# The first two products of a four-layer trunk, begun chunk by chunk while x is being scaled

## The chip, the cores and the metric

One core of one Trainium2 chip runs the program. The metric is the device time of one execution in microseconds (us), as the median of several runs; less is better. TensorE (PE in the profile) multiplies matrices, its weight loads have rows of their own (PEld); VectorE is DVE, ScalarE is ACT, GpSimd is POOL. SyncE (SP) issues most transfers. Each engine takes its instructions in the order in which the program wrote them.

## What is computed

One step of a trunk of four layers over 128 context tokens and 512 latent tokens of width 1024. Each layer is a token mixer (attention, convolution, gated linear attention, attention again) and a gated FFN. Each of these has in front a norm and a modulation whose vectors come from a conditioning vector through a large matrix:

```python
for i in range(DEPTH):
    sh1, sc1, g1, sh2, sc2, g2 = adaln(cond, mod_w[i], mod_b[i])     # silu(cond) @ w + b, in six parts
    h = modulate(rms_norm(x, norm1_g[i]), sh1, sc1)                   # norm(x) * (1 + scale) + shift
    x = x + g1 * mixer(h)            # layer 0: attention, first step q, k, v = h @ w_qkv
    x = x + g2 * conv_ffn(modulate(rms_norm(x, norm2_g[i]), sh2, sc2))
```

## The kernel before

The tokens lie along the free dimension and the 1024 channels in 8 chunks of 128 partitions. A product is written as three: x and each weight are split into a rounded high part and a low rest (`xh`, `xl`, `wh`, `wl`), and for each chunk `proj` (line 207) issues six matmuls, two column halves of 320 and 322 by high times high, low times high, high times low. A product over 8 chunks is 48 matmuls into one of two PSUM tiles, `mm0` and `mm1`.

The norm's factor per token is applied after the product, so what stands in `xh` and `xl` is only x times `A`, a vector per channel (`1 + scale` times the norm's gain), and two more columns, 0 and 129, that hold the shift of the context and of the latent tokens. The product's columns 0 and 129 are then the shift's image, which is added as a bias after the norm's factor.

The program is one list of tasks (`build`, line 1648), each written out in turn for all engines. It begins thus: eight tasks `mod_unit` multiply the conditioning by the eight parts of the matrix that give the scale, four small matmul columns each in `b`; `mod_end` copies, transposes and sums the result, and forms `A`. Then `first_norm` scales all eight chunks of x (`fin`, line 257: ScalarE writes `xh`, DVE writes `xl`, ScalarE squares x and POOL or DVE adds the squares into `acc`). Then come eight `mod_unit` tasks for the shift, and `first_shift` writes the shift columns. Then `attention` (line 636) opens: for each of 8 pairs of heads the products q, k, v, one task each (`project`), with one more `mod_unit` of the coming vectors between them. Behind the first product stand the ones matmuls that sum the squares over the partitions, and the norm's factor (`norm_rstd`); each q and k is then normed over its head, for which TensorE sums the squares once more (`sb<-N,blk`).

Matrices come through a ring of four raw buffers `wr` in the order in which the tasks use them (`fill`, `advance`). x itself comes in four transfers, on the same queue, behind the eight of the scale. A weight is converted into a ring of four half buffers `wh` and `wl` (two halves make one weight): ScalarE casts, and DVE or, in attention, POOL subtracts. `advance` is called in the middle and at the end of each product and converts one more half ahead, if its buffer is not to be read any more by a matmul that is still to be written:

```python
wait = self.turn >= self.NWS and self.took[-self.NWS][0].left[self.took[-self.NWS][1]] > 0
if u >= get + need and (wait or limit == 0):
    return
```

Of the kernel before, what the change touches and what calls it, by code (L numbers as in the profile page):

```python
# [25 lines left out]
NCH = 8  # L26
# [99 lines left out]
class Trunk:  # L126
# [129 lines left out]

    def fin(self, j, A, rolled):

        nc = self.nc
        for src, dst, g in self.pieces(self.x[:, j], self.xh[:, j], rolled):  # L260
            nc.scalar.activation(out=dst, in_=src, func=AF.Copy, scale=A[:, j, g:g + 1])
        for (src, dst, g), (_, hi, _) in zip(self.pieces(self.x[:, j], self.xl[:, j], rolled),
                                             self.pieces(self.x[:, j], self.xh[:, j], rolled)):
            nc.vector.scalar_tensor_tensor(out=dst, in0=src, scalar=A[:, j, g:g + 1], in1=f32(hi), op0=ALU.mult,  # L264
                                           op1=ALU.subtract)
        self.square(j)

# [165 lines left out]

    def first_norm(self, perm):
        self.lane_a.drain()
        for j in range(NCH):
            self.fin(j, self.A[0], perm)

    def first_shift(self):
        self.lane_a.drain()  # L440
        self.shift_cols(self.mod[0][0][:])
        self.advance(0, 0, 2)

# [191 lines left out]

    def attention(self, layer, la):

# [254 lines left out]
        def project(w, p, which, first):  # L892
# [5 lines left out]
            if (which, p) == ("v", NCH - 1):  # L898
                self.lane_a.add(early())
            self.proj(pm, w, self.xmv, NCH, True)  # L900
            if first:
                self.norm_rstd(True, (S.SB, S.PB))
# [57 lines left out]
        for p in range(NCH):  # L960
            for w, which in enumerate("qkv"):
                main.append(Task(lambda w, p=p, which=which: project(w, p, which, p == 0 and which == "q"),
                                 [("w", self.i["w_qkv"][la, 3 * p + w])]))
        tasks = [self.open(f"att{layer}", build)]
        tasks += self.weave(main, self.mod_tasks(layer, [2, 3, 4]))
        tasks.append(Task(gap))
# [681 lines left out]
    def build(self, stack):  # L1648
# [4 lines left out]
        T += scale[:4] + [Task(self.load_x)] + scale[4:]  # L1653
        T.append(Task(lambda: self.first_norm(True)))
        T += self.mod_tasks(0, [0])
        T.append(Task(self.first_shift))
        na = 0
        for layer in range(self.depth):
            kind = layer % 3
            if kind == 0:  # L1660
                T += self.attention(layer, na)
                na += 1
# [138 lines left out]
```

## Time and profile before

| what | value |
|---|---|
| median of 3 runs | 3420.74 us (3420.28 to 3421.49) |
| the profiled execution | 3424.34 us, of which the span of its trace 3422.6 us |
| TensorE busy | 3325.3 us, 97% |
| VectorE, ScalarE, GpSimd busy | 58%, 49%, 19% |
| granted clock of TensorE, mean over the span | 0.989 of 2.4 GHz |

A share of the span is a mean over stages with different limits. The change touches the first 60 us of the program, so the rows below are nearly all of these. The granted clock is given in parts of 2.4 GHz: 0.50 is 1.2 GHz. In a timeline row the first number is the start, the second the busy time of the row's instructions, and the bracket at the end the idle time ahead of it with what ended it.

### The profile page before, as it was taken

The numbers are of one execution on the slowest core, as the hardware profiler recorded it, in microseconds if no ns is written. First come the engines' busy times: TensorE is split into PE (matmuls) and PEld (weight loads), VectorE is DVE, ScalarE is ACT, GpSimd is POOL, SyncE is SP. The second block draws the span as 40 slices with busy tenths as digits, with TensorE's granted clock in tenths as the row PEclk, the third lists the DMA queues.
The fourth block names the chain that finished last, engine by engine and source line by source line (L and its number), as shares of the span: only waits on it lengthen the run. The fifth ranks groups of instructions, "written<-read, shape, count | busy, mean of one in ns | idle before, by whom it ended". The sixth has DMA issues, their size and how long they took to land.

```text
span 3422.6 us, 58735 instructions
## 1 busy us (share of the span) xinstructions
PE 3325.3 (97%) x23852; PEld 3105.8 (91%) x23852; DVE 2002.1 (58%) x3395; ACT 1662.0 (49%) x3200; POOL 657.1 (19%) x597
## 2 busy tenths in 40 slices
PE   6999999999999899999999999999999999999999
PEld 4888899999977799999988899999998888999999
DVE  4555666465567666465566676646565555664654
ACT  5666555343413454343455555534357665543433
POOL 4443310000135210000233441000024443200000
PEclk8999999999999899999999999999999999999999
DMA  6333233332265333222332223333223333232222
GB/s 219 114 116 109 76 100 105 104 105 82 90 178 165 108 100 111 99 69 76 104 102 84 91 64 107 105 111 105 74 94 117 109 111 95 83 106 79 71 74 74
DMA packets 110928, 349.74 MB, mean 102 GB/s; under 512 B 14496, under 2 KB 19680, under 8 KB 110656
## 3 DMA queue, kind: packets, MB, share of 16 engines
q1 hardware_dynamic: 107856, 340.15, 31.0%
q0 software_dynamic: 2416, 5.13, 0.4%
q8 instruction: 188, 3.08, 0.4%
q10 hardware_dynamic: 384, 0.69, 0.1%
q14 instruction: 84, 0.69, 0.1%
HBM read 329.13 MB, written 5.77 MB: 98 GB/s over the span
## 4 chain that ended last, share of the span: by engine, by line
PE 59%; DVE 4%; ACT 4%; issue 1%; POOL 1%; DMA 0%; SPq 0%; DVEq 0%; ACTq 0%; POOLq 0%
PE mm L222 7%; PE mm L226 6%; PE mm L224 6%; PE mm L227 6%; PE mm L225 6%; PE mm L223 6%; PE ax L222 2%; PE ax L226 2%; PE ax L225 2%; PE ax L224 2%; PE ax L227 2%; PE ax L223 2%; PE b L342 1%; PE at L1451 1%; ACT Q L747 1%
## 5 line engine op out<-in xcount | busy, mean ns | idle before, releaser
L171 DVE TENSOR_TENSOR wl<-wr,wh 128x512 fp32r<-128x512 f32 (+1 forms) x555 | 387.9, 703 | 658.2 <-ACT wh L170 657.7
L170 ACT CAST wh<-wr 128x512 fp32r<-128x512 f32 (+2 forms) x802 | 472.7, 597 | 612.3 <-PE mm L225 335.9
L222 PE MATMUL mm<-xh,wh 128*128 128x320 f32 x1791 | 594.8, 332 | 5.7 <-ACT wh L170 3.1
L226 PE MATMUL mm<-xh,wl 128*128 128x320 f32 x1791 | 557.8, 311 | 2.8 <-POOL wl L171 2.8
L224 PE MATMUL mm<-xl,wh 128*128 128x320 f32 x1791 | 557.0, 311 | 3.6 <-DVE xl L264 2.4
L225 PE MATMUL mm<-xl,wh 128*128 128x322 f32 (+1 forms) x1791 | 558.5, 312 | 0.0
L223 PE MATMUL mm<-xh,wh 128*128 128x322 f32 (+1 forms) x1791 | 556.8, 311 | 0.0
L227 PE MATMUL mm<-xh,wl 128*128 128x322 f32 (+1 forms) x1791 | 556.7, 311 | 0.0
L171 POOL TENSOR_TENSOR wl<-wr,wh 128x512 fp32r<-128x512 f32 (+2 forms) x247 | 319.3, 1298 | 606.7 <-ACT wh L170 514.7
L222 PEld LDWEIGHTS mm<-xh,wh 128*128 128x128 f32 x1791 | 338.5, 189 | 68.1 <-issue 48.6
L223 PEld LDWEIGHTS mm<-xh,wh 128*128 128x128 f32 x1791 | 342.1, 191 | 5.9
L224 PEld LDWEIGHTS mm<-xl,wh 128*128 128x128 f32 x1791 | 338.5, 189 | 5.0 <-DVE xl L264 3.5
L226 PEld LDWEIGHTS mm<-xh,wl 128*128 128x128 f32 x1791 | 339.0, 189 | 3.4 <-POOL wl L171 3.4
L227 PEld LDWEIGHTS mm<-xh,wl 128*128 128x128 f32 x1791 | 341.6, 191 | 0.0
L225 PEld LDWEIGHTS mm<-xl,wh 128*128 128x128 f32 x1791 | 340.3, 190 | 0.0
L287 POOL TENSOR_TENSOR acc<-acc,T 128x640 f32<-128x640 f32 x40 | 64.9, 1622 | 1428.3 <-ACT T L285 1416.1
L491 ACT ACTIVATE U<-T,D 128x128 f32<-128x128 f32 x176 | 71.2, 405 | 503.2 <-DVE D L490 503.2
L797 ACT ACTIVATE T<-T,sm 128x512 f32<-128x512 f32 x128 | 92.7, 724 | 148.3 <-DVE sm L793 148.0
L500 ACT ACTIVATE y<-U,ffc 128x641 f32<-128x641 f32 x176 | 161.7, 919 | 0.0
L503 DVE SCALAR_TENSOR_TENSOR y<-U,ffc,y 128x641 f32<-128x641 f32 x176 | 156.4, 889 | 7.0
L502 DVE SCALAR_TENSOR_TENSOR y<-U,ffc,y 128x641 f32<-128x641 f32 x176 | 156.4, 889 | 3.6
L222 PE MATMUL ax<-xh,wh 128*128 128x320 f32 x480 | 150.4, 313 | 0.0
(377 smaller groups left out, 7465.7 us busy)
## 6 DMA issues: line engine op xcount, KB each, us to landing
wr<-in_mod_w SPq DMA_DIRECT2D x192, 512.0 KB, 4.3
wr<-in_w_up SPq DMA_DIRECT2D x176, 512.0 KB, 3.5
wr<-in_w_down SPq DMA_DIRECT2D x64, 448.0 KB, 3.4
wr<-in_w_qkv SPq DMA_DIRECT2D x48, 512.0 KB, 4.6
bias<-in_bias SPq DMA_DIRECT2D x64, 256.0 KB, 2.7
wr<-in_w_down SPq DMA_DIRECT2D x32, 512.0 KB, 3.7
cr<-cu SPq DMA_DIRECT2D x120, 84.0 KB, 3.0
wr<-in_w_ao SPq DMA_DIRECT2D x16, 512.0 KB, 3.9
```

Of the source, the lines that this page charges most:

```text
L170: self.nc.scalar.copy(out=h, in_=src[:, a:a + n])
L171: self.lo_eng[self.turn % len(self.lo_eng)].tensor_tensor(out=l, in0=src[:, a:a + n], in1=f32(h), op=ALU.subtract)
L222: mm(oa, wh, ha, start=st, stop=False)
L223: mm(ob, wh, hb, start=st, stop=False)
L224: mm(oa, wh, la, start=False, stop=False)
L225: mm(ob, wh, lb, start=False, stop=False)
L226: mm(oa, wl, ha, start=False, stop=en)
L227: mm(ob, wl, hb, start=False, stop=en)
L500: nc.scalar.activation(out=y[:], in_=u[:, 1:642], func=AF.Identity, scale=c[:, 2:3], bias=c[:, 4:5])
L502: stt(out=y[:], in0=u[:, 0:641], scalar=c[:, 1:2], in1=y[:], op0=ALU.mult, op1=ALU.add)
L503: stt(out=y[:], in0=u[:, 2:643], scalar=c[:, 3:4], in1=y[:], op0=ALU.mult, op1=ALU.add)
L797: nc.scalar.activation(out=st[:, a * w:a * w + w], in_=src[:, a * w:a * w + w], func=AF.Exp, bias=sm[:, 2 + a:3 + a], accum_out=R[:, a:a + 1])
```

## The change

`first_norm` and `first_shift` give way to `first_products`. It zeroes the two shift columns and scales chunks 0 and 1 (`zeros`), takes the weights of q and k of the first pair of heads (`begin`), and then, for each chunk k, scales chunk k + 2, multiplies chunk k by both weights (`chunk`), and does one `mod_unit` of the shift. When the shift vector is there, `columns` writes the shift columns and multiplies columns 0 to 129 again by both weights. `attention` gets the dictionary `s` of `first_products` as `done`. When it writes its list of tasks it asks whether `done` is true; where it is, it leaves out q and k of the first pair and adds a task `head` that goes on from the products in `done`. `s` gets its entries in `begin`, when the tasks are run. The body of `project` behind `proj` has become `projected`. `fin` has a new argument `square` that no call sets.

```diff
--- before.py
+++ after.py
@@ -431,15 +432,54 @@
         for j in range(0, NCH, 2):
             self.nc.sync.dma_start(out=self.x[:, j:j + 2], in_=self.i["x"][:, j:j + 2])
-    def first_norm(self, perm):
-        self.lane_a.drain()
-        for j in range(NCH):
-            self.fin(j, self.A[0], perm)
-    def first_shift(self):
-        self.lane_a.drain()
-        self.shift_cols(self.mod[0][0][:])
-        self.advance(0, 0, 2)
+    def first_products(self, perm, units, shift):
+        s = {}
+        def begin(*ws):
+            s["w"], s["pm"] = ws, [self.next_mm() for _ in ws]
+            for w in ws:
+                w.left = [2 * n for n in w.left]
+        def chunk(k):
+            if k + 2 < NCH:
+                self.fin(k + 2, self.A[0], perm)
+            for w, pm in zip(s["w"], s["pm"]):
+                self.proj(pm, w, self.xmv, NCH, True, ks=[k])
...
+        def columns():
+            self.lane_a.drain()
+            self.shift_cols(self.mod[0][0][:])
+            mm = self.nc.tensor.matmul
+            g = slice(0, 130)
+            for w, pm in zip(s["w"], s["pm"]):
+                o = pm[:, 192:322]
+                for k in range(NCH):
+                    wh, wl = w.at(k)
+                    xh, xl = self.xh[:, k, g], self.xl[:, k, g]
+                    mm(o, wh, xh, start=(k == 0), stop=False)
+                    mm(o, wh, xl, start=False, stop=False)
+                    mm(o, wl, xh, start=False, stop=(k == NCH - 1))
+                self.advance(0, 0, 2)
+        def zeros():
+            self.lane_a.drain()
+            g = slice(0, 130, 129)
+            for t in (self.xh, self.xl):
+                self.nc.vector.memset(f32(t[:, :, g]), 0.0)
+            for j in range(2):
+                self.fin(j, self.A[0], perm)
+        tasks = [Task(zeros), Task(begin, [("w", u) for u in units])]
+        for k in range(NCH):
+            tasks.append(Task(lambda k=k: chunk(k)))
+            tasks.append(shift[k])
+        return tasks + [shift[NCH], Task(columns)], s
     def open(self, name, build):
         def go():
@@ -633,7 +673,7 @@
         return tasks
-    def attention(self, layer, la):
+    def attention(self, layer, la, done=None):
         S = type("S", (), {})()
@@ -898,6 +938,22 @@
             if (which, p) == ("v", NCH - 1):
                 self.lane_a.add(early())
             self.proj(pm, w, self.xmv, NCH, True)
+            projected(pm, p, which, first)
+        def head(done):
+            start_pair(0)
+            load_pair(0)
+            pq, pk = done["pm"]
+            self.norm_rstd(True, (S.SB, S.PB))
+            gq, gk = normed(pq, "q", 0), normed(pk, "k", 0)
+            next(gq)
+            next(gk)
+            gk = self.after(gq, gk)
+            self.lane_a.add(gq)
+            self.lane_a.add(gk)
+            self.lane_b.add(self.after(gk, units(0)))
+        def projected(pm, p, which, first):
             if first:
                 self.norm_rstd(True, (S.SB, S.PB))
             g = values(pm, p) if which == "v" else normed(pm, which, p)
@@ -959,9 +1015,13 @@
         main = []
         for p in range(NCH):
             for w, which in enumerate("qkv"):
+                if done and p == 0 and which != "v":
+                    continue
                 main.append(Task(lambda w, p=p, which=which: project(w, p, which, p == 0 and which == "q"),
                                  [("w", self.i["w_qkv"][la, 3 * p + w])]))
         tasks = [self.open(f"att{layer}", build)]
+        if done:
+            tasks.append(Task(lambda: head(done)))
         tasks += self.weave(main, self.mod_tasks(layer, [2, 3, 4]))
         tasks.append(Task(gap))
         for g in range(2):
@@ -1651,14 +1711,13 @@
         T.append(Task(self.begin))
         scale = self.mod_tasks(0, [1])
         T += scale[:4] + [Task(self.load_x)] + scale[4:]
-        T.append(Task(lambda: self.first_norm(True)))
-        T += self.mod_tasks(0, [0])
-        T.append(Task(self.first_shift))
+        tasks, done = self.first_products(True, [self.i["w_qkv"][0, j] for j in range(2)], self.mod_tasks(0, [0]))
+        T += tasks
         na = 0
         for layer in range(self.depth):
             kind = layer % 3
             if kind == 0:
-                T += self.attention(layer, na)
+                T += self.attention(layer, na, None if layer else done)
                 na += 1
             elif kind == 1:
                 T += self.conformer(layer)
```

How the instructions stand in the two programs is seen at three places.

TensorE, from the transposes of the scale vector on (`b<-ident,modrow`). Before, eight shift units (`b<-wr,cond`, of which the first two and the last stand here), the transposes of the shift, and the first product:

```order
L354 MATMUL b_124<-ident,modrow 128x128 x2
L342 MATMUL b_124<-wr_66,cond 32x256 x4
L342 MATMUL b_124<-wr_67,cond 32x256 x4
...
L342 MATMUL b_124<-wr_69,cond 32x256 x4
L354 MATMUL b_124<-ident,modrow 128x128 x2
L222 MATMUL mm_122<-xh,wh_70 128x320
L223 MATMUL mm_122<-xh,wh_70 128x322
L224 MATMUL mm_122<-xl,wh_70 128x320
```

With the change, at the same place (`mm_122` and `mm_123` are the two PSUM tiles, `wh_70` and `wh_72` halves of the two weights):

```order
L355 MATMUL b_124<-ident,modrow 128x128 x2
L222 MATMUL mm_122<-xh,wh_70 128x320
...
L226 MATMUL mm_122<-xh,wl_74 128x320
L227 MATMUL mm_122<-xh,wl_74 128x322
L222 MATMUL mm_123<-xh,wh_72 128x320
...
L226 MATMUL mm_123<-xh,wl_76 128x320
L227 MATMUL mm_123<-xh,wl_76 128x322
L343 MATMUL b_124<-wr_68,cond 32x256 x4
L222 MATMUL mm_122<-xh,wh_70 128x320
```

Twelve matmuls, one chunk by two weights, now stand ahead of each shift unit, and the units have moved behind them.

TensorE again, from the end of the first product of attention on. Before:

```order
L226 MATMUL mm_122<-xh,wl_75 128x320
L227 MATMUL mm_122<-xh,wl_75 128x322
L301 MATMUL sb<-acc,ones 128x320
L301 MATMUL pb<-acc,ones 128x320
L342 MATMUL b_124<-wr_67,cond 32x256 x4
```

With the change, from the last shift unit on, in three pieces: the transposes and the first of the 48 column matmuls (`128x130`); the last of these and the product that follows; the end of that product and what is behind it:

```order
L343 MATMUL b_124<-wr_67,cond 32x256 x4
L355 MATMUL b_124<-ident,modrow 128x128 x2
L465 MATMUL mm_122<-xh,wh_70 128x130
...
L465 MATMUL mm_123<-xh,wh_73 128x130
L466 MATMUL mm_123<-xl,wh_73 128x130
L467 MATMUL mm_123<-xh,wl_77 128x130
L222 MATMUL mm_122<-xh,wh_70 128x320
...
L227 MATMUL mm_122<-xh,wl_75 128x322
L302 MATMUL sb<-acc,ones 128x320
L302 MATMUL pb<-acc,ones 128x320
L343 MATMUL b_124<-wr_69,cond 32x256 x4
L222 MATMUL mm_123<-xh,wh_72 128x320
```

Behind the columns stand 48 matmuls of full width into `mm_122`, the ones matmuls, a `mod_unit` and a product into `mm_123`, as before from the first product on. TensorE has 144 matmuls more in all, and none less; from there to the end its rows are those of before.

ScalarE, from the copy of the shift vector's row on. Before:

```order
L350 COPY modrow<-b_124 128x256
L292 CAST xh<-mod_0_85 128x8x2
L170 CAST wh_70<-wr_66 128x512
...
L170 CAST wh_72<-wr_68 128x512
L170 CAST wh_73<-wr_68 128x512
L306 ACT_TABLE_LOAD
L316 ACTIVATE T_80<-sb,eps 128x320
```

With the change, with the engines that a row waits for:

```order
L351 COPY modrow<-b_124 128x256 [waits PE_49]
L293 CAST xh<-mod_0_85 128x8x2 [waits DVE_49]
L170 CAST wh_70<-wr_68 128x512 [waits DMAHW6_49,PE_49]
...
L170 CAST wh_72<-wr_66 128x512 [waits DMAHW0_49,PE_49]
L170 CAST wh_73<-wr_66 128x512 [waits PE_49]
L170 CAST wh_70<-wr_68 128x512 [waits DMAHW2_49,DVE_49,PE_49]
L170 CAST wh_71<-wr_68 128x512 [waits DVE_49,PE_49]
L307 ACT_TABLE_LOAD
L317 ACTIVATE T_80<-sb,eps 128x320 [waits PE_49]
L317 ACTIVATE T_80<-pb,eps 128x320 [waits PE_49]
```

Between the shift columns (`xh<-mod`) and the table load there are now six casts where there were four, in buffers that matmuls have read (they wait for PE), and the last two are of the weight after next. SP has two loads of 512 KB more (`in_w_qkv`, the two weights of `begin`), which stand ahead of the shift's eight; DVE has four more low halves `wl` there, and two that POOL had.

## Rows read from the trace of the kernel before

**Rows 1.** The page, part 1: busy time of TensorE, share of the span, instructions.

```profile
PE 3325.3 (97%) x23852; PEld 3105.8 (91%) x23852; DVE 2002.1 (58%) x3395; ACT 1662.0 (49%) x3200; POOL 657.1 (19%) x597
```

**Rows 2.** Windows: stretch, length, busy us of five engines, granted clock, DMA share, GB/s.

```profile
24.00:34.00 10.00, 7.56 (x56) 1.42 (x56) 10.00 (x9) 10.00 (x19) 8.52 (x5) 0.50 0.98 356
41.00:46.00 5.00, 5.00 (x19) 5.00 (x20) 2.19 (x7) 2.57 (x4) 2.51 (x2) 0.50 0.57 192
47.00:52.00 5.00, 5.00 (x35) 4.40 (x37) 0.00 (x0) 0.55 (x2) 0.00 (x0) 1.00 0.00 0
```

**Rows 3.** Timeline of TensorE, 16 to 69 us.

```profile
16.32 1.08 PE L342 MATMUL b<-wr,cond 128*32 128x256 f32 x8 [0.18 <-DMA wr<-in_mod_w]
...
40.78 0.63 PE L222 MATMUL mm<-xh,wh 128*128 128x320 f32 x1 [3.15 <-ACT wh L170]
41.21 0.47 PE L223 MATMUL mm<-xh,wh 128*128 128x322 f32 x1
...
46.83 0.33 PE L226 MATMUL mm<-xh,wl 128*128 128x320 f32 x1
...
50.70 0.70 PE L301 MATMUL sb<-acc,ones 128*128 128x320 f32 x2
...
51.87 0.64 PE L342 MATMUL b<-wr,cond 128*32 128x256 f32 x8
52.44 0.42 PE L222 MATMUL mm<-xh,wh 128*128 128x320 f32 x1
...
58.72 0.41 PE L301 MATMUL sb<-N,blk 128*128 128x320 f32 x1 [1.47 <-POOL N L705]
...
62.60 0.42 PE L222 MATMUL mm<-xh,wh 128*128 128x320 f32 x1
...
68.61 0.42 PE L301 MATMUL sb<-N,blk 128*128 128x320 f32 x1 [1.20 <-POOL N L705]
```

**Rows 4.** Timeline of DVE, 18 to 42 us.

```profile
18.68 0.17 DVE L360 TENSOR_TENSOR mod<-b,modb 128x16 f32<-128x16 f32 x1 [16.72 <-PE b L354]
...
37.69 1.47 DVE L264 SCALAR_TENSOR_TENSOR xl<-x,A,xh 128x128 fp32r<-128x128 f32 x3
...
39.80 0.17 DVE L360 TENSOR_TENSOR mod<-b,modb 128x16 f32<-128x16 f32 x1
...
40.76 1.29 DVE L171 TENSOR_TENSOR wl<-wr,wh 128x512 fp32r<-128x512 f32 x2 [0.31 <-ACT wh L170]
```

**Rows 5.** Timeline of ScalarE, 40 to 52 us.

```profile
40.01 0.22 ACT L292 CAST xh<-mod 128x16 fp32r<-128x16 f32 x1 [3.11 <-DVE mod L360]
40.12 2.17 ACT L170 CAST wh<-wr 128x512 fp32r<-128x512 f32 x4
42.31 1.28 ACT L306 ACT_TABLE_LOAD   x1
51.44 0.53 ACT L316 ACTIVATE T<-sb,eps 128x320 f32<-128x320 f32 x1 [7.85 <-PE sb L301]
```

**Rows 6.** Timeline of SP's queue, 13 to 14 us.

```profile
13.23 0.50 SPq L145 DMA_DIRECT2D wr<-in_mod_w  x1
```

**Rows 7.** DMA issues of the same microsecond: the last number is us to landing.

```profile
wr<-in_mod_w SPq DMA_DIRECT2D x1, 512.0 KB, 10.7
```

**Rows 8.** Timeline of TensorE, small matmuls in the first attention.

```profile
106.17 0.56 PE L816 MATMUL sb<-K,Q 128*128 128x128 f32 x4
106.56 0.36 PE L222 MATMUL mm<-xh,wh 128*128 128x320 f32 x1
...
109.42 0.61 PE L854 MATMUL ob<-PT,V 128*64 128x128 f32 x8
109.96 0.66 PE L841 MATMUL pb<-ident,T 128*128 128x128 f32 x4
```

**Rows 9.** Waits of ScalarE, 75 to 400 us: total us, times, longest.

```profile
ACT T L797 <- DVE sm L793: 81.3, 59, 2.9
```

More of the change, by code (lines that the diff above doesn't have):

```diff
@@ L255, in pieces, with fin @@
         return out + [(a[:, 0:56], b[:, 8:64], 1), (a[:, 56:64], b[:, 0:8], 1)]
-    def fin(self, j, A, rolled):
+    def fin(self, j, A, rolled, square=True):
         nc = self.nc
@@ L265, in fin @@
                                            op1=ALU.subtract)
-        self.square(j)
+        if square:
+            self.square(j)
     def fins(self, j, sh):
@@ L432, in load_x, with squares @@
             self.nc.sync.dma_start(out=self.x[:, j:j + 2], in_=self.i["x"][:, j:j + 2])
-    def first_norm(self, perm):
-        self.lane_a.drain()
-        for j in range(NCH):
-            self.fin(j, self.A[0], perm)
-    def first_shift(self):
-        self.lane_a.drain()
-        self.shift_cols(self.mod[0][0][:])
-        self.advance(0, 0, 2)
+    def first_products(self, perm, units, shift):
[9 more added lines that the diff above has]
+                self.proj(pm, w, self.xmv, NCH, True, ks=[k])
+        def squares():
+            for j in range(NCH):
+                self.square(j)
+        def columns():
[24 more added lines that the diff above has]
+        return tasks + [shift[NCH], Task(columns)], s
     def open(self, name, build):
```

## The prediction

> **What bounds the kernel now.** The page first: TensorE is busy 97% of the span [rows 1], so an edit that adds products to it, or moves them to where it must idle, shows in the time; all else matters only where TensorE waits for it. Stages second: of 24 to 34 us TensorE is busy 7.56 of 10 us, all of it in the small matmuls that make the shift vector, at a granted clock of 0.50; at 41 to 46 us it runs products without a gap, still at 0.50; from 47 us it has 1.00 and keeps it [rows 2]. Then its timeline [rows 3]. The first product starts at 40.78, after an idle stretch, and 22 of its 48 matmuls run at the half clock, (46.83 - 41.21) / 21 = 0.268 us apart; the other 26 are (50.70 - 46.83) / 26 = 0.149 apart. What held the start is DVE and then ScalarE: DVE forms the low half of the last chunk from 37.69, adds a square, and only then builds the shift vector at 39.80 [rows 4]; ScalarE rounds it into the shift columns at 40.01 and converts the first weight at 40.12 [rows 5]. So about 22 us in which x is being scaled (19 to 41) hold no product at all, and that is where the change puts some.
>
> **What the change does, part by part.** It matters first what it does not do. The order of the built kernel keeps the whole q product and the whole k product behind the column matmuls: `first_products` returns an empty dictionary when the list of tasks is written, `attention` tests it for truth at that time, takes the same branch as before, and the tests that would drop q and k and add `head` never fire. So 96 + 48 matmuls are added and none is removed: 8 chunks of 12, and 48 of 130 columns. Two loads of 512 KB, four casts on ScalarE and four low halves (two of them that POOL did before now on DVE besides) come with them. The question is how much of that lies under the wait before 40.78.
>
> *When the early products can begin.* The two weights are now the loads that the first two shift units were. The first of those was issued at 13.23 [rows 6] and took 10.7 us to land [rows 7]: 23.9. A cast is 0.61 (2.17 for four with overlap, [rows 5]), so TensorE starts at 24.6, the low half (1.29 for two, [rows 4]) following in time for the fifth matmul but for some 0.3.
>
> *How long they take.* A chunk is 12 products and one shift unit. At the half clock that is 12 x 0.268 + 1.08 (the last scale unit's row) = 4.3 us; at the full clock 12 x 0.149 + 0.57 (51.87 to 52.44) + 0.1 for the slower first product behind it (0.42 in its row, 0.33 at 46.83) = 2.46. The chunks come faster than the half clock can use them and about as fast as the full clock can: DVE ended the last chunk at 37.69 + 1.47 = 39.2; with four more low halves at 0.65 it ends at 41.8 at the latest. So TensorE itself sets the pace. In the trace the clock rose 6.05 us after the first product; I take the same here: 30.65. Then: chunk 0 from 24.6 to 28.2, its shift unit to 29.3, five products of chunk 1 at the half clock to 30.65, seven at the full clock and a unit to 32.3, six more chunks at 2.46 = 14.8, to 47.1.
>
> *The shift units' loads.* On SP they now stand behind the two weights. The third and fourth go into the buffers of these and wait for DVE's low halves, so for about 27; each later one waits for the unit four before it on TensorE, four chunks or some 10 us ahead of its use, about what a load took at its slowest [rows 7]. The third is used at 34: with 10.7 us to land it would hold TensorE 3 us. But the 10.7 came from x's four loads queued ahead of it, which are landed by then; I take 0 of 0 to 3.
>
> *The tail of the shift vector, now bare.* Before, the copy, the transposes and the sum hid under DVE's last chunk. Now they follow the last shift unit: the scale vector's chain shows the price, 16.32 + 1.08 = 17.40 to 18.68 for the sum, 0.21 more to the rounding (39.80 to 40.01), 0.22 for it: 1.7 us. The columns begin at 48.8.
>
> *The columns.* No row has 130 columns in this type. The nearest is four matmuls of 128 columns with 128-column weights: 106.17 to 106.56, 0.0975 each [rows 8]; 48 of them are 4.7 us. Below it stand eight with half as many weight columns, 109.42 to 109.96, 0.0675 each, so 3.2; above it the full-width product at 0.149, so 7.2. I take 4.7, nearest in shape: q starts at 53.5, against 40.78. The Trainium skill (TensorE: Matmul & The Clock Gate, section on LDWEIGHTS) puts a weight load at the number of its columns over 1.2 GHz, whatever is streamed; as an estimate that makes 0.107 each, 5.1 in all instead of 4.7, 0.4 us more against the change.
>
> *What comes back.* q now runs at the full clock: 48 x 0.149 = 7.15, done at 60.7, where the ones matmul stood at 50.70 before. That is +10.0: a start 12.7 later, and 9.92 - 7.15 = 2.8 of product time less.
>
> *Two waits behind it.* ScalarE's order now has a table load (1.28) behind two casts that overwrite q's own weight buffers, so they wait for q's last reads; before, the load was done by 43.6. Behind it are the logarithms of the norm, which started at 51.44, 0.74 after the ones began [rows 5]. The new chain is: last read some 0.15 before the ones, cast 0.55, table 1.28, so 1.7 after the ones began: +1.0. TensorE waits for the end of this chain already (1.47 at 58.72 [rows 3]), so all of it counts. The second such wait (1.20 at 68.61) grows by at most a cast, 0.6, because the next cast too now waits for the product that is running; I take 0.3.
>
> *The rest.* Through the first mixer each weight is now converted one product further ahead, into a buffer that the running product has just left. ScalarE idles there anyway (81.3 us in 59 waits for the softmax between 75 and 400 us [rows 9]) and the casts stand where they stood, so I price it at 0; if every one of some 42 casts held the queue 0.2 us and TensorE with it, it would be 8. The instruction orders run together again before the first FFN, so nothing lasts to the end.
>
> Sum: +10.0 + 1.0 + 0.3 = +11.3 us. The profiled execution took 3424.34 (span 3422.6), 3.6 above the median of the runs, 3420.74; the early stretch has no reason to differ between them, so the sum goes on the median: **3432.0**. What a measurement of this kernel can tell from no change is about 0.2%, 6.8 us, so this is a small loss that shows.
>
> **The rivals.**
> A, the forecast: the clock rises within 27 to 34 us, columns at 0.0675 to 0.149. Own range +8.5 to +15.5: 3429 to 3436. Chance 0.70.
> B, the clock stays at the half for most of the early products, because a shift unit stands between every twelve of them. For it: from 24 to 34 us TensorE was 76% busy with such units and stayed at 0.50 [rows 2]. Against it: the products fill the rest, with hardly a gap. If it lasts to the last chunk, eight chunks end at 24.9 + 8 x 4.3 = 59.3, the columns start at 61.0, take some 7 with the clock rising in them, q ends at 75.2: +24.5, and +1.3: 3446.5. Halfway, 3439. Chance 0.13. The Trainium skill (same page, Part 1) calls the slow clock the default that sustained matmul activity releases; by that rule B would be short, and the rise at 46.83 agrees, while the shift units alone did not bring it.
> C, the casts that are a product ahead do hold up TensorE in the first mixer: +11.3 + 8 = 3440. Against it: ScalarE's idle time there. Chance 0.06.
> D, not slower: the early products cost almost nothing, because the clock is up from the first of them and the columns cost as little as the half-width weights. Then DVE's last chunk at 41.8 and TensorE's own 24.9 + 8 x 2.46 = 44.6 leave columns at 46.3 to 49.5, q done at 56.7: +6.0, +1.3 = 3428.0, on the edge; it turns to no change when columns start before 45.8. Nothing in the rows has the clock up before sustained products. Chance 0.09, two thirds of it within 0.2%.
> E, faster: the products made early are used and q and k are not repeated. Then v could start at 53.5 instead of 62.60, 9.1 earlier: 3411.6. The built order shows both products again, so 0.02.
>
> **How the numbers follow.** Slower: A, B, C and a third of D, 0.70 + 0.13 + 0.06 + 0.03 = 0.92, less 0.02 for a short A: 0.90. Same: 0.06 + 0.02 = 0.08. Faster: E, 0.02. The range reaches from D's lower part, 3427, to the middle of B, 3441, and leaves out the long B and E.
>
> **What would show it.** Right: first products near 24.6; the clock at 1.00 by about 31; the last shift unit near 47; 48 short matmuls of some 4.7 us in all; q's 48 products after them at 1.00; the ones near 60.7, and a table load of 1.28 between q's end and the logarithms, with the wait at the norm's sums 2.5 instead of 1.47. From there to the end the same length, within 1 us. Wrong: a clock at 0.50 past 35 us, columns far from 0.1 apart, TensorE waiting for DVE between early chunks, new waits on weights between 75 and 400 us, or q and k missing behind the columns.

## The result, and the profile after

The changed kernel takes 3436.86 us (median of 6 runs, 3432.58 to 3441.73). The kernel before, run between them on the same chip, takes 3420.51. The ratio is 1.0051, with a 95% interval of 1.0041 to 1.0061: slower, by more than the 0.2% that a measurement can tell.

The profiled execution of the changed kernel took 3436.02, with a span of 3434.2 against 3422.6 before, so it is 11.6 longer. That is less than the 16.3 (3436.86 - 3420.51) between the medians, and the difference matters below. The page shows TensorE with its 144 additional matmuls, none fewer [rows 1]:

```profile
PE 3342.1 (97%) x23996; PEld 3123.6 (91%) x23996; DVE 2004.7 (58%) x3403; ACT 1665.7 (49%) x3204; POOL 652.9 (19%) x595
```

The timeline of TensorE from the first early product to the second product of attention (start, busy us, in the bracket the idle time ahead and what ended it) answers to [rows 3]:

```profile
24.45 0.63 PE L222 MATMUL mm<-xh,wh 128*128 128x320 f32 x1 [5.99 <-ACT wh L170]
24.88 0.47 PE L223 MATMUL mm<-xh,wh 128*128 128x322 f32 x1
25.14 0.47 PE L224 MATMUL mm<-xl,wh 128*128 128x320 f32 x1
...
28.93 0.31 PE L223 MATMUL mm<-xh,wh 128*128 128x322 f32 x1
29.08 0.30 PE L224 MATMUL mm<-xl,wh 128*128 128x320 f32 x1
...
46.28 0.64 PE L343 MATMUL b<-wr,cond 128*32 128x256 f32 x8
47.41 0.44 PE L355 MATMUL b<-ident,modrow 128*128 128x128 f32 x2 [0.49 <-ACT modrow L351]
48.44 0.33 PE L465 MATMUL mm<-xh,wh 128*128 128x130 f32 x1 [0.59 <-ACT xh L293]
...
49.16 0.28 PE L467 MATMUL mm<-xh,wl 128*128 128x130 f32 x1
49.27 0.27 PE L465 MATMUL mm<-xh,wh 128*128 128x130 f32 x1
...
53.96 0.36 PE L222 MATMUL mm<-xh,wh 128*128 128x320 f32 x1
...
61.10 0.70 PE L302 MATMUL sb<-acc,ones 128*128 128x320 f32 x2
...
62.84 0.42 PE L222 MATMUL mm<-xh,wh 128*128 128x320 f32 x1
...
67.91 0.41 PE L302 MATMUL sb<-N,blk 128*128 128x320 f32 x1 [0.40 <-ACT N L743]
70.09 0.42 PE L302 MATMUL sb<-N,blk 128*128 128x320 f32 x1 [1.77 <-POOL N L745]
```

Read it by its distances. The early products are 0.27 apart at first (the half clock) and 0.15 from 28.93 on. The last shift unit starts at 46.28 and ends at 46.9. Up to the columns TensorE then has only the two transposes, with 0.49 idle ahead of them and 0.59 behind; these 1.5 us are called the pause below. The columns begin at 48.44 and stand 0.111 apart, q begins at 53.96 and the ones stand at 61.10, where 50.70 stood before. The second product starts 10.40 later than before (62.84 against 52.44), and the norm's sums wait 0.40 + 1.77 instead of 1.47.

Between these two executions nothing is lost or won after that. A row of DVE early in the first mixer, and its last one there, before:

```profile
79.19 0.69 DVE L785 CUSTOM_DVE_ANT_0 T<-sb,bias 128x512 f32<-128x512 f32 x1 [2.06 <-issue]
...
441.89 1.41 DVE L929 SCALAR_TENSOR_TENSOR x<-mm,mod,x 128x128 f32<-128x128 f32 x2
```

and the same instructions after:

```profile
91.02 0.69 DVE L825 CUSTOM_DVE_ANT_0 T<-sb,bias 128x512 f32<-128x512 f32 x1 [1.69 <-issue]
...
453.74 1.41 DVE L985 SCALAR_TENSOR_TENSOR x<-mm,mod,x 128x128 f32<-128x128 f32 x2
```

The shift is 11.83 and 11.85, and 11.6 at the end of the span. The whole loss of this execution arises in the first 91 us (79 before). That the rest is equally long in these two, 2980.7 us before and 2980.5 after, is in part chance: from the same row to the end, the fourteen profiled executions of this document take between 2973.9 and 2980.7 us.

### The profile page after: what moved, and what is told of

The parts are those of the page before. It is cut to its first block, busy times and chain, and to the rows that moved or that the text cites. A ratio compares the mean times of both kernels' runs of the same rounds, so it can differ in the third digit from the quotient of the medians.

```text
span 3434.2 us, 59054 instructions
## 1 busy us (share of the span) xinstructions
PE 3342.1 (97%) x23996; PEld 3123.6 (91%) x23996; DVE 2004.7 (58%) x3403; ACT 1665.7 (49%) x3204; POOL 652.9 (19%) x595
## 4 chain that ended last, share of the span: by engine, by line
PE 59%; DVE 4%; ACT 4%; issue 1%; POOL 1%; DMA 0%; SPq 0%; DVEq 0%; ACTq 0%; POOLq 0%
PE mm L222 7%; PE mm L226 6%; PE mm L224 6%; PE mm L227 6%; PE mm L225 6%; PE mm L223 6%; PE ax L222 2%; PE ax L226 2%; PE ax L225 2%; PE ax L224 2%; PE ax L227 2%; PE ax L223 2%; PE b L343 1%; ACT Q L787 1%; PE at L1511 1%
## 5 line engine op out<-in xcount | busy, mean ns | idle before, releaser
L171 DVE TENSOR_TENSOR wl<-wr,wh 128x512 fp32r<-128x512 f32 (+2 forms) x561 | 392.2, 704 | 663.2 <-ACT wh L170 662.3
```

The lines of the kernel that those rows point to most:

```text
L171: self.lo_eng[self.turn % len(self.lo_eng)].tensor_tensor(out=l, in0=src[:, a:a + n], in1=f32(h), op=ALU.subtract)
```

## The experiments

The theory: the early products are thrown away, so what is left of the change is a q that starts later, by the shift vector's bare tail and 48 column matmuls. Rivals: the casts that are a product ahead; the clock; a table load that doesn't matter. Twelve runs were made on three chips, one of them of the changed kernel again; each is set against the kernel before on the same chip, and that with half the columns is a single execution.

**The products kept, first try.** The test is mended, and two `mod_unit` tasks stand behind `head`, where v now is the first product:

```diff
-                if done and p == 0 and which != "v":
+                if done is not None and p == 0 and which != "v":
...
-        if done:
+        extra = self.mod_tasks(layer, [2, 3, 4])
+        if done is not None:
             tasks.append(Task(lambda: head(done)))
-        tasks += self.weave(main, self.mod_tasks(layer, [2, 3, 4]))
+            tasks, extra = tasks + extra[:2], extra[2:]
+        tasks += self.weave(main, extra)
```

Expected:

> The products made early are kept: q and k of pair 0 are not multiplied again, and the head of the pair (norm, q and k normalised) stands in their place. My theory is that the loss comes only from the repeated products; then v can start right behind the columns at about 54 us instead of q, the ones follow at 54 to 55, and the span is 3 to 9 us below that of the kernel before (3411 to 3417 us), about 20 below the changed one. A rival, that the new order itself (casts, loads, small shift units between products) is what costs, leaves the time at or above that of the kernel before, 3420 or more, though 96 matmuls fewer run than in the changed kernel.

Measured: 3487.4 against 3419.45, ratio 1.0199 (1.0186 to 1.0213). The theory's time failed; the rival's (3420 or more) came out, but not by its cause. The waits of TensorE from 60 to 430 us (engine, line, what it waited for: us in all, times, longest) say where:

```profile
PE ob L894 <- DMA Vc<-in_vc: 37.0, 6, 6.5
PE sb L812 <- DVE sm L825: 7.9, 7, 3.3
```

`head` lets k's normalising wait for the end of q's (`after(gq, gk)`). So the attention of pair 0 begins later: its first scores (`sb<-K,Q`) stand 29.2 us behind the start of v (87.17 - 57.93), in the kernel before 15.8 (78.44 - 62.60), while the products of the next pairs come no later. The cached values lie in a ring of two buffers. The load of pair 2's is issued at 118.03, and pair 0's products with that buffer (`ob<-PT,Vc`) run until 137.07; in the kernel before the load is issued at 126.89, behind the last of them at 113.30. So the attention of the latent tokens reads buffers that have been refilled, and this kernel doesn't compute what the others do. Six times TensorE waits for such a load, some 6 us each. So the mended test alone would not have made the change pay.

**The products kept, second try.** The first steps of both chains are taken at once, and k follows q by two steps (`behind` yields twice and then goes on with `gk`):

```diff
-            next(gq)
-            next(gk)
-            gk = self.after(gq, gk)
+            for g in (gq, gk, gq, gk, gq):
+                next(g)
+            gk = self.behind(2, gk)
```

Expected:

> The early products are kept, as in the first such kernel, but the head lets the normalising of k follow that of q by two steps instead of waiting for its end, and takes the first steps of both at once, so that the attention of pair 0 begins as many steps ahead of pair 2 as in the kernel before. Theory: nothing of the mixer is late then, v starts at 56 to 58 instead of 62.60 (columns' end 54, ones and two small units 2 us, perhaps a wait), q's sums cost a wait of 2 to 3, and the time is 1 to 6 us below the kernel before (ratio 0.998 to 1.000). Rival: the lanes stay late as in the first such kernel (waits of the products on the cached values' loads), 20 us or more above.

Measured: 3416.77 against 3420.3, ratio 0.9992 (0.9983 to 1.0000). The time is as expected, though the interval just reaches no change, and the waits on cached values are gone. But v starts at 63.53 in its trace, not at 56 to 58. The 11 runs fall into two groups, four from 3421.17 to 3421.40 and seven from 3411.11 to 3417.14, and the profiled one, 3421.34, is of the upper group. In it the columns begin 0.111 apart and go on at 0.213 from 51.3 on. So part of v's delay is a clock that fell; that this makes the two groups is not shown, since no execution of the lower one was profiled.

**No columns.** The result of the columns is thrown away in the changed kernel, so it stays complete without them:

```diff
-                o = pm[:, 192:322]
-                for k in range(NCH):
...
-                    mm(o, wl, xh, start=False, stop=(k == NCH - 1))
+                w.left = [0 for n in w.left]
                 self.advance(0, 0, 2)
```

Expected:

> The changed kernel without the 48 column matmuls; their results are thrown away in it, so the output stays complete. If the columns cost what their pitch in the trace says (0.111 x 48 = 5.5 us), q starts 5.5 us earlier, near 48.5, and the time is 5 to 6 us below the changed kernel. If ScalarE, DVE or a weight is what lets q start, the time falls by under 2 us.

Measured: 3427.76, ratio 1.0025 (1.0015 to 1.0035). Against the changed kernel's 1.0051 that is some 9 us less, not 5 to 6. So the 5.5 us of the trace above seem not to be what the columns cost in most executions. In its trace q starts behind a wait for the cast of a weight, 4.9 earlier and not 5.5:

```profile
49.07 0.41 PE L222 MATMUL mm<-xh,wh 128*128 128x320 f32 x1 [1.09 <-ACT wh L170]
...
50.23 0.47 PE L227 MATMUL mm<-xh,wl 128*128 128x322 f32 x1
50.50 0.47 PE L222 MATMUL mm<-xh,wh 128*128 128x320 f32 x1
...
53.14 0.31 PE L226 MATMUL mm<-xh,wl 128*128 128x320 f32 x1
```

From 49.8 to 53.1 q's products are 0.27 apart: here the clock falls too, but for 3.3 us only.

**No early products, no columns.** Two loads, four casts, the low halves and the order of the shift units stay:

```diff
-            for w, pm in zip(s["w"], s["pm"]):
-                self.proj(pm, w, self.xmv, NCH, True, ks=[k])
```

Expected:

> The changed kernel without the early products and without the columns; the two extra loads, the four casts, the low halves, the shift units between the chunks and the order of the squares stay. My theory (TensorE's serial work behind the early products makes the loss) puts q at 42 to 44 us, at the half clock, and the time 1 to 4 us above the kernel before. The rival that the order of casts and loads costs through the first mixer leaves it 8 or more above. If the clock matters more than the products, so that early products pay for themselves by the clock, this kernel is no faster than the one without columns alone.

Measured: 3425.64, ratio 1.0017 (1.0009 to 1.0026). q starts at 43.41, as expected, but the 6.2 us between the medians (3 to 9 by the interval) are more than the 1 to 4 expected. The trace says where they are: q and the ones stand 2.6 later than before, the norm's sums that waited for the table load 3.6 (62.28 against 58.72), and behind them the clock is at the half from 63.2 to 66.4; the first DVE row of the mixer shown above is 5.5 later (84.73 against 79.19). It lies 2.1 below the kernel without columns, which the intervals do not separate: the early products themselves cost little on top of the new order, and whether the clock that they bring pays for them this run can't tell.

**The table load at the start.** One line behind the Silu in `begin`:

```diff
         nc.scalar.activation(out=self.cond[:, :, 0:2], in_=self.condr[:], func=AF.Silu)
+        self.table(EXPLN)
```

Expected:

> The changed kernel with one table load more, at the program's start behind the Silu, so that the load of 1.28 us between q's end and the norm's logarithms should go. Theory: that load stands on the path, the wait of TensorE at the norm's sums (0.40 + 1.77 in the changed kernel) falls by 1.0 to 1.3 us and so does the time. Rival: POOL's part of the norm ends last there, then the wait and the time stay within 0.3 us.

Measured: 3434.39, ratio 1.0045 (1.0032 to 1.0059): 2.5 below the first median of the changed kernel, which the intervals do not separate. The logarithms start 0.74 behind the ones, as before, instead of 1.83, and the first norm wait is 1.47 again: from the second product to these sums it is 6.27 us (69.52 to 75.79), in the changed kernel 7.25 (62.84 to 70.09), before 6.28 (52.44 to 58.72). So the load did stand on the path, for 1.0 us. But the trace also holds what the one above does not. TensorE in the columns:

```profile
49.57 0.27 PE L466 MATMUL mm<-xh,wh 128*128 128x130 f32 x1
49.68 0.32 PE L467 MATMUL mm<-xl,wh 128*128 128x130 f32 x1
49.80 0.41 PE L468 MATMUL mm<-xh,wl 128*128 128x130 f32 x1
50.02 0.41 PE L466 MATMUL mm<-xh,wh 128*128 128x130 f32 x1
```

From 49.8 on they are 0.213 apart: the clock fell, some 1 us behind the pause. A new theory follows: the bare tail costs not only its own length, it sometimes takes the clock away too.

**The pause filled.** Twelve full-width products, thrown away, in TensorE's pause (`filler` multiplies chunk 7 by the weight of q again):

```diff
         def columns():
+            filler(3)
             self.lane_a.drain()
+            filler(9)
             self.shift_cols(self.mod[0][0][:])
```

Expected:

> The changed kernel with 12 more products of full width in TensorE's pause behind the last shift unit (3 ahead of the two transposes, 9 behind them); what they give is overwritten later, and the order of the rest stays. They take 1.8 us at the full clock of the 2.1 us in which TensorE had only the transposes. Clock theory: in some runs the clock falls to the half behind this pause (as in the run with the table load, where the columns then took 0.213 each), which costs 5 to 7 us in those runs; with the pause filled it stays up, the time is 2 to 5 us below the changed kernel (ratio to before near 1.0035 instead of 1.0051) and the runs lie closer together, and every column stands 0.111 behind the one before. Rival: the clock falls for another reason, or the spread comes from later stretches; then the time is that of the changed kernel or up to 0.5 us above it.

Measured: 3433.85, ratio 1.0044 (1.0031 to 1.0056); in its trace the columns are 0.111 apart throughout. The pause is 1.5 us by the rows, not the 2.1 of the expectation, so the fillers also move the columns 0.6 later, to 49.02. The size is as the clock theory has it, but the interval overlaps that of the changed kernel, so by its time alone this run decides nothing.

**The tail two chunks earlier.** Copy, transposes and sum of the shift vector move under chunks 6 and 7:

```diff
             tasks.append(Task(lambda k=k: chunk(k)))
-            tasks.append(shift[k])
-        return tasks + [shift[NCH], Task(columns)], s
+            if k < NCH - 2:
+                tasks.append(shift[k])
+            if k == NCH - 3:
+                tasks += shift[k + 1:]
+        return tasks + [Task(columns)], s
...
+            if k == NCH - 1:
+                self.lane_a.drain()
```

Expected:

> The changed kernel with the last two shift units and the shift vector's end two chunks earlier, so that copy, transposes and sum lie under chunks 6 and 7 of the products; only the rounding into the shift columns is left behind the last product. Theory: of the 2.1 us of pause 1.5 go, and with the pause the fall of the clock: 3 to 6 us below the changed kernel, ratio to before near 1.003. Rival (a load of a shift unit now comes too late and holds TensorE, or the clock falls all the same): no faster than the changed kernel.

Measured: 3431.58, ratio 1.0037 (1.0024 to 1.0050). The columns start at 47.30 behind a wait of 0.16, at the full clock. The median is 5.3 below the first one of the changed kernel, within the expected 3 to 6, but the intervals overlap. The profiled execution, 3436.31, is the slowest of the five: its ones stand 1.15 earlier than in the changed kernel (59.95 against 61.10), and then the clock falls behind the norm's wait of 1.77, from 69.5 to 72.9, which takes it back.

**The pause longer, the same pause filled, and the changed kernel again.** These three ran on one chip. The first adds five copies on ScalarE ahead of the rounding, the second adds the same copies and 23 products:

```diff
         def columns():
+            filler(3)
             self.lane_a.drain()
+            filler(20)
+            for _ in range(5):
+                self.nc.scalar.copy(out=self.T.next()[:, 0:512], in_=self.x[:, 7, 0:512])
             self.shift_cols(self.mod[0][0][:])
```

Expected of the pause alone, without the `filler` lines:

> The changed kernel with five copies of 0.6 us on ScalarE (into scratch, not used) ahead of the rounding into the shift columns, so that TensorE pauses some 2.2 us longer ahead of the columns. Clock theory: the longer pause brings the clock to the half in every run; the columns then take 0.213 each instead of 0.111 and q begins at the half clock, 6 to 7 us on top of the 2.2, so 6 to 9 us above the changed kernel in the median (some of its runs fall already), runs close together. Rival (the fall has nothing to do with the pause): 2.2 us above the changed kernel, the spread as it was.

Expected of the filled pause:

> The same five copies, and 23 products of full width on TensorE in the pause (thrown away later), so that the columns start as late as with the copies alone, but TensorE works till then. Clock theory: the columns go 0.111 apart in the trace and q at the full clock; 5 to 7 us below the kernel with the pause alone, and 0 to 2 us above the changed kernel. Rival: the same time as with the pause alone, within 1 us.

Expected of the changed kernel:

> The changed kernel once more, beside the two with the longer pause, on the same chip. Clock theory: the clock falls behind its pause in some runs and not in others, so its median lies between that of the filled pause less 2 us and that of the pause alone less 2 us, and its runs are spread over 5 us or more. Rival: runs as close together as those of the kernel before on this chip.

Measured: 3440.62 with the pause (ratio 1.0062, 1.0049 to 1.0074), 3434.51 with the pause filled (1.0043, 1.0030 to 1.0057), 3442.12 for the changed kernel (1.0064, 1.0051 to 1.0076). The two with the copies start their columns within 0.2 of each other (50.32 and 50.49). Windows of the pause alone (stretch, length, busy us of PE, PEld, DVE, ACT and POOL, granted clock, DMA share, GB/s):

```profile
48.00:50.00 2.00, 0.04 (x1) 0.00 (x0) 0.18 (x1) 2.00 (x5) 0.00 (x0) 1.00 0.83 231
50.00:52.00 2.00, 1.68 (x8) 1.69 (x9) 0.19 (x1) 0.26 (x2) 0.00 (x0) 0.51 0.13 53
52.00:54.00 2.00, 2.00 (x11) 2.00 (x11) 0.37 (x1) 0.62 (x1) 0.00 (x0) 0.50 0.00 0
```

and of the filled pause:

```profile
48.00:50.00 2.00, 2.00 (x15) 2.00 (x15) 0.07 (x1) 1.90 (x5) 0.00 (x0) 1.00 0.64 227
50.00:52.00 2.00, 2.00 (x19) 2.00 (x18) 0.12 (x1) 0.13 (x1) 0.00 (x0) 1.00 0.02 8
52.00:54.00 2.00, 2.00 (x20) 2.00 (x20) 0.83 (x2) 1.11 (x2) 0.00 (x0) 1.00 0.00 0
```

With the pause empty, 11 column matmuls stand in the last 2 us at clock 0.50; with it filled, 20 at 1.00. Filling it with useless work gains 6.1 us in the median, in the expected 5 to 7, and the runs of the two don't overlap (3439.20 to 3442.04, 3433.58 to 3436.78). In the traces the ones stand at 69.16 and 62.93, 6.2 apart: the fall is caused by the pause, for the longer pause. What was expected against the changed kernel failed: on this chip, at 3442.12, it lies above the 3432.5 to 3438.6 that its expectation comes to, 1.5 above the kernel with the longer pause and 7.6 above the filled one. So on this chip the shorter pause seems to have had the fall in most runs; only one of them was profiled. Their spread (5.1 us) tells nothing, since the kernel before has 8.3 on this chip.

Its trace is telling, since it is of the same program as the one shown in the result:

```profile
46.11 0.64 PE L343 MATMUL b<-wr,cond 128*32 128x256 f32 x8
47.24 0.44 PE L355 MATMUL b<-ident,modrow 128*128 128x128 f32 x2 [0.49 <-ACT modrow L351]
48.27 0.33 PE L465 MATMUL mm<-xh,wh 128*128 128x130 f32 x1 [0.59 <-ACT xh L293]
...
49.22 0.28 PE L466 MATMUL mm<-xl,wh 128*128 128x130 f32 x1
49.33 0.33 PE L467 MATMUL mm<-xh,wl 128*128 128x130 f32 x1
49.46 0.42 PE L465 MATMUL mm<-xh,wh 128*128 128x130 f32 x1
49.68 0.41 PE L466 MATMUL mm<-xl,wh 128*128 128x130 f32 x1
...
57.78 0.57 PE L222 MATMUL mm<-xh,wh 128*128 128x320 f32 x1
...
67.31 0.70 PE L302 MATMUL sb<-acc,ones 128*128 128x320 f32 x2
...
76.30 0.42 PE L302 MATMUL sb<-N,blk 128*128 128x320 f32 x1 [1.77 <-POOL N L745]
...
76.95 0.47 PE L222 MATMUL mm<-xh,wh 128*128 128x320 f32 x1
...
80.15 0.32 PE L222 MATMUL mm<-xh,wh 128*128 128x320 f32 x1
```

Up to 49.33 it is the other trace, 0.17 earlier. Then the clock falls: the columns take 57.78 - 48.27 = 9.5 instead of 5.5 (which answers to the 9 us that the kernel without them gains), q starts at the half clock and has the full one again only from 63.0 on, and the ones stand at 67.31 instead of 61.10, 6.2 later. The clock is low for 13.5 us here, and for 13.4 to 13.7 with the table load, half the columns and the longer pause, where column matmuls followed as well; without columns it was 3.3, and q took 1.65 longer (57.86 - 49.07 = 8.79 for 7.14). So the 6.2 are the price of a fall with the columns behind it; whether it is they that keep the clock low, one trace without them doesn't show. Behind the norm's wait of 1.77 it falls once more: two chunks of the next product take 80.15 - 76.95 = 3.20. Counted from that product's first chunk, this is 1.4 more than the 1.78 (70.64 to 72.42) of the other trace. With that the two executions are 7.7 apart at the next shift unit (81.13 and 73.39), and their spans differ by 7.6 (3441.8 and 3434.2).

This second fall is no exception. Of the nine traces with the norm's wait of 1.76 or 1.77, which is what the table load makes of 1.47, seven show it (no columns, no early products, half the columns, the pause filled, the earlier tail, the longer pause filled, and this one); the first trace of the changed kernel and that of the longer pause do not. Neither do the kernel before and that with the early table load, where the wait is 1.47.

**Half the columns.** Each column matmul streams 64 columns instead of 130:

```diff
-            g = slice(0, 130)
+            g = slice(0, 64)
...
-                o = pm[:, 192:322]
+                o = pm[:, 192:256]
```

Expected:

> The changed kernel with 64 columns streamed by each of the 48 column matmuls instead of 130; the recomputed columns 64 to 129 are left out, so the result is not complete. If loading the 128x128 weights sets the pace (the Trainium skill, TensorE: Matmul & The Clock Gate, section on LDWEIGHTS, puts it at 128 columns over 1.2 GHz, 0.107), the matmuls stay 0.105 to 0.112 apart at the full clock. If the streaming of the columns sets it, they come at half the distance or little more, 0.055 to 0.07.

Measured, in one execution: 3441.51 (it had the fall). Its columns, ahead of the fall:

```profile
49.01 0.28 PE L465 MATMUL mm<-xh,wh 128*128 128x64 f32 x1
49.13 0.28 PE L466 MATMUL mm<-xl,wh 128*128 128x64 f32 x1
49.24 0.28 PE L467 MATMUL mm<-xh,wl 128*128 128x64 f32 x1
```

They stay 0.11 apart, and 0.213 at the half clock. So the streamed columns don't set the pace, and fewer of them gain nothing. That the weight load does is not shown by this run alone; it fits the matmuls with half as many weight columns, 0.0675 apart [rows 8].

**All together.** The second try with the kept products, with the early table load, the earlier tail, and the norm's ones ahead of the last chunk (`open` makes attention's buffers, `norm` is the `norm_rstd` that stood in `head`):

```diff
             if k == NCH - 1:
                 self.lane_a.drain()
+                s["open"].fn()
+                s["norm"]()
```

Expected:

> The kept products with three more moves: the table load at the start, the shift vector's end two chunks earlier, and the norm's sums ahead of the last chunk. Theory: columns start near 47 to 48 at the full clock, v at 54 to 55 against 62.60, no wait at the norm beyond what the kernel before has (1.47 + 1.20): 6 to 10 us below the kernel before, ratio 0.997 to 0.998. Rival: ScalarE and POOL, which normalise q and k together now, hold the sums by 4 us or more; then it is no better than 0.999.

Measured: 3410.96 against 3420.3, ratio 0.9972 (0.9963 to 0.9981): faster than both kernels, by as much as expected. In its trace the ones stand ahead of the last chunk of products, columns and v follow without a fall, and the norm's sums no longer hold TensorE by more than 0.33:

```profile
46.23 0.70 PE L307 MATMUL pb<-acc,ones 128*128 128x320 f32 x2
...
48.95 0.33 PE L475 MATMUL mm<-xh,wh 128*128 128x130 f32 x1 [0.25 <-ACT xh L298]
...
54.57 1.07 PE L348 MATMUL b<-wr,cond 128*32 128x256 f32 x16
55.58 0.42 PE L227 MATMUL mm<-xh,wh 128*128 128x320 f32 x1
...
58.96 0.42 PE L307 MATMUL sb<-N,blk 128*128 128x320 f32 x1 [0.33 <-POOL N L758]
...
70.47 0.33 PE L825 MATMUL sb<-ident,A 128*128 128x128 f32 x1 [1.82 <-ACT A L815]
```

v starts at 55.58 instead of 62.60 [rows 3], 0.6 behind the expected 54 to 55. A wait of 1.82 at v's transposes is new against the kernel before, and behind it the clock is at the half from 71.7 to 75.3. What each of the three moves gives on the kept products by itself was not run.

## Why the prediction was right or wrong

The direction and the cause came out as forecast: the early products are not used, and the delay of q makes the loss. So did the time of the profiled execution: +11.6 stands against the forecast sum of +11.3. The median, 3436.86, is inside the range but 4.9 above the point. Term by term:

- *First products near 24.6*: 24.45.
- *Clock up by 30.65*: the last products 0.27 apart end at 28.1, and the shift unit there takes 0.56 instead of 1.08, so 2.5 us earlier.
- *A chunk 2.46 at the full clock*: 18.2 / 7 = 2.6 (28.68 to 46.85); in one of them TensorE also waits 0.2 for a low half of DVE's. This takes back about what the early clock gave, so the end of the last shift unit is right by two errors that cancel.
- *Last shift unit's end 47.1, tail 1.7, columns at 48.8*: 46.28 + 0.64 = 46.9, tail 1.5, 48.44.
- *Columns 4.7 us*: 53.96 - 48.44 = 5.5, 0.111 each. The row taken, 0.0975 [rows 8], was too low. The Trainium skill (TensorE: Matmul & The Clock Gate, section on LDWEIGHTS) makes 0.107 of it, an estimate from its formula, which has the weight's columns in it and not the streamed ones; the 0.111 is nearer to it than to the row, and the run with 64 columns agrees. At the half clock the rows give 0.213, twice its figure, and there they decide.
- *q at the full clock, ones at 60.7*: 61.10 - 53.96 = 7.14 against 7.15, ones at 61.10, so +10.4 for +10.0.
- *Table load +1.0, second wait +0.3*: the idle time ahead of the first sums grew from 1.47 to 0.40 + 1.77, and from the second product's start to them it is 7.25 instead of 6.28, +1.0, which goes when the load moves to the start. From there to the second sums it is 10.34 (70.09 to 80.43) instead of 9.89, +0.45, of which the wait itself has 0.1. The three add up: 10.4 + 1.0 + 0.45 = 11.8, the shift in the mixer.
- *The rest 0*: 11.83 and 11.85 at both ends of the mixer. Rival C is out.

That the sum goes on the median, because "the early stretch has no reason to differ" between executions, is the step that did not hold, and under it "q now runs at the full clock" and the same assumption under the columns: once the clock was up, it was taken to stay up. The prediction reads "from 47 us it has 1.00 and keeps it" out of a window that ends at 52 [rows 2]. The page of the kernel before had a fall in it, in slice 14 of 40 (1112 to 1198 us) of its clock row:

```profile
PEclk8999999999999899999999999999999999999999
```

I had priced the bare tail as 1.7 us of time and not asked what TensorE does in it, and the longer wait at the norm's sums as 1.0 us of time. Rival B was about the clock, but about one that doesn't rise; none was about one that falls again. Of eight profiled executions with early products and a pause behind the last shift unit (the changed kernel twice, the two tries with kept products, no columns, the table load, half the columns, the longer pause), six show the fall there and two do not. None of the four without the pause does (filled twice, the earlier tail, all together). The fall costs 6.2, the second one 1.4, so the loss is 11.6 in an execution with neither and 19.2 (3441.8 - 3422.6) in one with both. The first six runs, at +12.1 to +21.2, span about that. Which of them had a fall isn't known, except that the profiled one had none. It lies near their median all the same, because its later part is of the longest kind; so is that of the profiled execution before, 3.8 above its own median. So the nearness of +11.6 to +11.3 rests in part on the luck of which executions were profiled.

The Trainium skill (same page, Part 1) says of the rise of the clock that its place varies from run to run of the same kernel. The two traces of one program show such a difference in a fall: one has it at 49.46, the other not at all.

Open: why the fall seems more frequent in one set of runs than in the other; why the second set of the changed kernel lies 22.9 above the kernel before on its chip (3442.12 - 3419.27), 3.6 more than both falls explain; and what the up to 7 us of difference in the later part are. The traces of all these kernels show falls of the clock between 1000 and 1240 us too; that these make the difference is not shown.

## What to carry to other kernels

A serial chain that is laid bare costs its length and, where it leaves TensorE with nothing but two transposes for as little as 1.5 us, perhaps the clock of what comes after: here 6.2 us for a pause of 1.5 ahead of the columns, in some executions only, and 1.4 for a wait that grew to 1.77. Compare several executions before a small sum is called right, and look at the distances of the matmuls behind each pause. And a product taken out of a pipeline of steps shifts everything that counts its steps: the mended test alone made the kernel 2% slower, with buffers refilled too early; with the chain beside it moved to match it was at most 0.2% faster, and clearly faster (0.3%) only with the tail, the table load and the norm moved too.

## What was not expected of the hardware

Behind the pause of 1.5 us the fall doesn't show in the first instruction: the columns had already run 1.1 to 1.9 us without a gap when they slowed down (48.27 to 49.4 in the trace above, 49.44 to 51.3 in the second try with the kept products), and without columns q 0.75. Behind the longer pause the first column is already at the half clock. The recorded clock is not reliable at the start of a trace: the changed kernel's windows give 1.00 from 24 to 28 us, where the products stand 0.267 apart, the distance that they have at 0.50 elsewhere [rows 2, 3].
